# A hybrid decoder step on one core: three buffers for the weights' sums, written order on three engines, the first products of two units ahead

## The chip, the cores and the metric

The kernel runs on one core of a Trainium2 chip. The metric is the device time of one execution in microseconds (us), taken as the median of several runs. TensorE is called PE here, VectorE DVE, ScalarE ACT, GpSimd POOL and SyncE SP, as the profile names them. SP issues plain loads; POOL issues the loads that add to what is in memory already.

## The reference, cut to what matters

Two layers over 544 tokens (512 of a prompt and 8 times 4 of samples), model width 1024, all in float32. Each layer has two feed-forward blocks (FFN), so the step has four; between them stand a recurrent block, a shared key and value projection and differential attention. An FFN is the place of the change:

```python
def rmsnorm(x, g):
    xf = x.astype(jnp.float32)
    y = xf * lax.rsqrt(jnp.mean(xf * xf, axis=-1, keepdims=True) + EPS) * g.astype(jnp.float32)
    return y.astype(x.dtype)

def swiglu(x, w_gu, w_down):
    g, u = jnp.split(x @ w_gu, 2, axis=-1)
    return (jax.nn.silu(g) * u) @ w_down
...
        x = x + 0.5 * swiglu(rmsnorm(x, W['ffn1_norm'][i]), W['ffn1_w_gu'][i], W['ffn1_w_down'][i])
```

The hidden width `D_FF` is 2816, that is 22 slices of 128.

## The kernel before

**Tiling.** Activations lie with the 1024 channels on the 128 partitions in 8 blocks and the 544 tokens along the row. A float32 product is made of three products in the format float32r: a value is split into a high part (ACT casts it) and a low part (DVE subtracts the high part), and high by high, high by low and low by high are summed in PSUM.

**Units.** In the FFN one of the 22 slices is a unit `f`. Its gate and up products are written as seven products of half size (a Strassen-like scheme), each of 4 blocks by 3 splits = 12 matmuls of 272 columns. `s0` to `s6` issue them: on PE the order in the middle of a group is `s6(f)`, `s0(f+1)`, `s1(f)`, `s2(f+1)`, `s3(f+1)`, `s4(f)`, `s5(f+1)`, `s6(f+1)`, 84 matmuls for a unit. The seven products need sums of quarters of the weights. Tile `r` holds them: SP loads two quarters into it, POOL loads two others on top with an adding DMA, then DVE adds the quarters in `x` (loaded into a tile `raw`) by `sum6` (L427) and `sum3` (L432). So each unit has three weight operands, x, y and z, that are split in turn: `raw` is x, `r[:, 0:2]` is y (after `sum6`), `r[:, 2:4]` is z (after `sum3`); a fourth, `a`, is split into `w4`. The split is ACT `wh` (L370) and DVE `wl` (L371). Splits use three buffers in turn for x, y and z; `r` has two buffers.

**What follows a product on DVE.** L460 reads the sum of `s1(f)` out of PSUM, and PE's `s4(f)` adds to the same place only after that. L479 follows `s3`, L485 `s4`, L507 `s6`; L490 and L492 make the hidden slice, `hh` and `hl`.

**Groups.** The 22 units stand in three groups of 8, 7 and 7 (`DOWN`). After the units of a group come the down products: 8 output blocks, 384 or 336 matmuls (L211).

**Order.** A planner walks through `steps` and asks for loads and splits some units ahead (`pump`, `may_load`). From the code that results, a scheduler sets each engine's order by readiness and priority, so that an engine's instructions don't stand as they were written; an engine then runs its own in that order, and one that waits holds back all behind it.

**Start of an FFN.** `first_cycle` interleaves the products of unit 0 block by block, and `norm_done` makes the token's norm: squares summed on DVE or POOL, two times two matmuls with ones, then a chain of small DVE operations (`rsqrt_rows`, 13 on 17 columns, with a transposition ahead and a copy and a transposition behind) that ends in `rb`.

Of the kernel before, what the change touches and what calls it, by code (L numbers as in the profile page):

```python
# [8 lines left out]
F32 = mybir.dt.float32  # L9
# [66 lines left out]
def trunk_kernel(ctx: ExitStack, tc: tile.TileContext, I, O):  # L76
# [179 lines left out]
    def rsqrt_rows(out, ss, n, count, tr=None):  # L256

        nb = n // 32
        np_ = out.shape[0]
        if ss is not None:  # L260
            tr = npool.tile([P, T], F32, tag="tr", name="tr", bufs=1)[:, :n]
            norm["read"] = dve.transpose(tr, ss)
# [18 lines left out]

    def norm_done():
        if not norm["old"]:
            return
        norm["old"] = False
        hi = npool.tile([P, T], F32R, tag="sq", name="acch", bufs=1)
        lo = npool.tile([P, T], F32R, tag="tr", name="accl", bufs=1)
        split(hi, lo, norm["acc"])
# [5 lines left out]
        norm["ins"] = rsqrt_rows(rb, body(ps), T, D)  # L294
        norm["rb"] = rb
# [68 lines left out]
    def ffn(l, which, gain_out, spill_x=False, beside=None):  # L364
# [3 lines left out]

        def late_low(hi, lo, src):
            act.copy(hi, src)  # L370
            later(lambda: dve.tensor_tensor(lo, src, hi.bitcast(F32), op=OP.subtract))  # L371

# [21 lines left out]
        def unit_y(f):  # L394
            src = wgu[l, f]
            u = U[f]

            def load():
                r = u["r"] = F["w"].tile([P, 4, 512], F32, tag="r", name="r")
                sp.dma_start(r[:, 0:4:2, :], src[:, 1:3, :])  # L400
                pool.dma_start(r[:, 0:4:2, :], src[:, 0:2, :], accum_op=OP.add)  # L401
                u["a"] = F["w"].tile([P, 512], F32, tag="a", name="a")
                sp.dma_start(u["a"], src[:, 0, :])

            def cut():
                sum6(f)
                hi, lo = pair()
                late_low(hi, lo, u["r"][:, 0:2, :].rearrange("p k n -> p (k n)"))
                return hi, lo

            return {"load": load, "split": cut, "open": lambda: F.get("w") is not None}

        def unit_z(f):
            u = U[f]

            def cut():
                sum3(f)
# [4 lines left out]
            return {"load": lambda: None, "split": cut, "open": lambda: True}  # L422

# [10 lines left out]
        def low4(f):  # L434
            u = U[f]
            u["w4"] = [F["w"].tile([P, 512], F32R, tag=n, name=n, bufs=1) for n in ("w4h", "w4l")]
            late_low(*u["w4"], u["a"])

# [16 lines left out]
        def s1(f):  # L455

            u = U[f]
            product(u["b"], 7, ready[u["iz"]], 0, first=False)
            t1 = u["t1"] = F["w"].tile([P, T], F32, tag="t1", name="t1")
            dve.tensor_tensor(t1[:, TH:], u["b"], u["cc"][:, 2], op=OP.add)  # L460
            dve.tensor_tensor(t1[:, TH:], t1[:, TH:], norm["rb"][:, TH:], op=OP.mult)  # L461
            finish()

        def s2(f):
            u = U[f]
            u["c"] = new_ps()[:, :TH]
            product(u["c"], 5, ready[u["iy"]], 0)
            act.copy(u["cc"][:, 2], u["c"])
# [40 lines left out]

        def first_cycle(f):  # L510

            u = U[f]
            begin(f)
            u["c"] = new_ps()[:, :TH]
            for k in range(KC // 2):
                product(u["b"], 1, ready[u["ix"]], 0, [k])
                product(u["c"], 5, ready[u["iy"]], 0, [k])
            act.copy(u["cc"][:, 0], u["b"])  # L518
            act.copy(u["cc"][:, 2], u["c"])
            for k in range(KC // 2):  # L520
                product(u["a_"], 2, ready[u["ix"]], 512, [k])
                product(u["c"], 3, ready[u["iz"]], 512, [k], first=False)
                product(u["b"], 6, ready[u["iy"]], 512, [k], first=False)
            up_first(f)
            finish()
            act.copy(u["cc"][:, 1], u["b"])
            finish()
            dve.tensor_tensor(u["t2"][:, TH:], u["c"], u["cc"][:, 1], op=OP.add)
            low4(f)
            norm_done()  # L530

# [46 lines left out]
        def group(a, b):  # L578
            H["a"], H["b"] = a, b
            if a == 0:  # L580
                hp, H["close"] = open_pool("ffnh", bufs=1, side="right")
                H["hh"] = hp.tile([P, KC, T], F32R, name="hh")
                H["hl"] = hp.tile([P, KC, T], F32R, name="hl")

        def step(fn, *args):
            add(None, lambda: fn(*args), -1)

        for part, (a, b) in enumerate(DOWN):
            for f in range(a, b):
# [4 lines left out]
                if f == 0:  # L594
                    step(first_cycle, 0)
                    continue
                step(s0, f)
                if f > a:
                    step(s1, f - 1)
                step(s2, f)  # L600
                step(s3, f)
                if f > a:
# [4 lines left out]
            add(wdn[l, 0][:, a:b, :], down(0, part))  # L607
            step(s4, b - 1)
            step(down_rest, part)
            for m in range(1, KC):  # L610
                add(wdn[l, m][:, a:b, :], down(m, part))

# [359 lines left out]
    def shared_kv():  # L972
# [36 lines left out]
        def vstep(nh, kk):  # L1009
            def go(wh, wl):  # L1010
# [13 lines left out]
                for c in range(5):  # L1024
                    vo = pp.tile([P, 512], F32, tag="vo", name="vo")
                    dve.tensor_scalar(vo, banks[c], B["rt"][:, c : c + 1], None, op0=OP.mult)
# [561 lines left out]
    def start():  # L1588
# [16 lines left out]
        for k in range(KC):  # L1605
# [3 lines left out]
            if k == 3:  # L1609
                units[1]["load"]()  # L1610
        units[0]["take"](first[0])
        at["dma"], at["split"] = 3, 1
# [7 lines left out]
        for k in range(KC):  # L1620
# [3 lines left out]
            if k == 6:  # L1624
                split_unit()
        for k in range(KC):
            square_in(k, pool if k in () else dve)
        pool.dma_start(ident, cst("ident"))
# [81 lines left out]
    def may_load():  # L1710
# [140 lines left out]
```

## Time and profile before

| | |
|---|---|
| runs | 2444.92, 2446.29, 2449.08 us; median 2446.29 |
| the profiled execution's own time | 2453.01 us |
| its span | 2451.2 us |
| PE busy | 2183.6 us (89%) |
| DVE busy | 1537.3 us (63%) |
| ACT busy | 1056.9 us (43%) |
| mean granted PE clock | 0.946 |

The span runs from the first to the last instruction. Busy time of PE counts matmuls that overlap, so that a busy PE need not be one at its peak; the granted clock, in parts of full speed, says how fast they could run. What stands in the idle time of an engine is told by what ended it.

### The profile page before, as it was taken

The numbers are of one execution on the slowest core, as the hardware profiler recorded it, in microseconds if no ns is written. First come the engines' busy times: TensorE is split into PE (matmuls) and PEld (weight loads), VectorE is DVE, ScalarE is ACT, GpSimd is POOL, SyncE is SP. The second block draws the span as 40 slices with busy tenths as digits, with TensorE's granted clock in tenths as the row PEclk, the third lists the DMA queues.
The fourth block names the chain that finished last, engine by engine and source line by source line (L and its number), as shares of the span: only waits on it lengthen the run. The fifth ranks groups of instructions, "written<-read, shape, count | busy, mean of one in ns | idle before, by whom it ended". The sixth has DMA issues, their size and how long they took to land.

```text
span 2451.2 us, 39182 instructions
## 1 busy us (share of the span) xinstructions
PE 2183.6 (89%) x15973; PEld 2097.4 (86%) x15973; DVE 1537.3 (63%) x2516; ACT 1056.9 (43%) x1635; POOL 292.8 (12%) x307
## 2 busy tenths in 40 slices
PE   6898998999889899899988989899869889989897
PEld 5798998999879899899878979899736879889797
DVE  6665656777765565678566556567745665565676
ACT  5333424498443333445244243343644443333444
POOL 1000000222100000011000000003331100000012
PEclk7899999999989999999999999999989889999999
DMA  6543534336344454323674354438983445453331
GB/s 175 122 128 99 144 96 113 106 103 166 96 121 133 114 133 111 99 90 103 206 229 125 111 127 128 116 96 246 228 252 93 104 121 147 103 136 104 98 106 65
DMA packets 135636, 318.10 MB, mean 130 GB/s; under 512 B 13920, under 2 KB 25968, under 8 KB 135328
## 3 DMA queue, kind: packets, MB, share of 16 engines
q1 hardware_dynamic: 102432, 240.20, 31.1%
q0 software_dynamic: 32336, 74.80, 16.4%
q8 instruction: 125, 2.05, 0.3%
q10 hardware_dynamic: 688, 0.60, 0.1%
q14 instruction: 55, 0.45, 0.1%
HBM read 285.38 MB, written 17.58 MB: 124 GB/s over the span
## 4 chain that ended last, share of the span: by engine, by line
PE 46%; DMA 30%; DVE 15%; issue 5%; ACT 3%; POOL 0%; SPq 0%; POOLq 0%; DVEq 0%; ACTq 0%
PE ps L211 29%; DMA r<-in_ffn_gu 25%; PE ps L359 11%; DVE wl L371 3%; DVE r L427 2%; DVE r L432 2%; PE ps L1020 1%; PE g L211 1%; DVE t L460 1%; DMA x<-in_cache_v,idx 1%; DVE t L461 1%; DMA wl<-raw 1%; DVE wl L221 1%; DVE xgl L233 1%; DMA vt<-vscr 1%
## 5 line engine op out<-in xcount | busy, mean ns | idle before, releaser
L359 PE MATMUL ps<-xgh,wh 128*128 128x272 f32 x1408 | 414.9, 295 | 21.1 <-ACT cc L518 10.3
L359 PE MATMUL ps<-xgl,wh 128*128 128x272 f32 x1408 | 412.7, 293 | 5.7 <-DVE xgl L233 5.6
L359 PE MATMUL ps<-xgh,wl 128*128 128x272 f32 x1408 | 413.1, 293 | 4.5 <-DVE wl L371 4.3
L359 PEld LDWEIGHTS ps<-xgh,wh 128*128 128x128 f32 x1408 | 272.1, 193 | 23.7 <-ACT wh L370 11.2
L211 PE MATMUL ps<-hh,wl 128*128 128x256 f32 (+1 forms) x1408 | 291.6, 288 | 0.0
L211 PE MATMUL ps<-hh,wh 128*128 128x256 f32 (+1 forms) x1408 | 291.1, 288 | 0.0
L211 PE MATMUL ps<-hl,wh 128*128 128x256 f32 (+1 forms) x1408 | 290.8, 288 | 0.0
L427 DVE TENSOR_TENSOR r<-r,raw 128x512 f32<-128x512 f32 x88 | 62.0, 705 | 355.2 <-DMA r<-in_ffn_gu 254.6
L401 POOL DMA_DIRECT2D r<-in_ffn_gu x88 | 106.4, 1209 | 1459.9 <-DMA r<-in_ffn_gu 778.5
L359 PEld LDWEIGHTS ps<-xgl,wh 128*128 128x128 f32 x1408 | 272.0, 193 | 7.1 <-DVE xgl L233 7.1
L359 PEld LDWEIGHTS ps<-xgh,wl 128*128 128x128 f32 x1408 | 271.4, 193 | 5.9 <-DVE wl L371 5.5
L220 ACT CAST wh<-raw 128x1024 fp32r<-128x1024 f32 (+3 forms) x158 | 150.3, 959 | 270.7 <-PE ps L211 187.9
L371 DVE TENSOR_TENSOR wl<-r,wh 128x1024 fp32r<-128x1024 f32 x176 | 214.8, 1221 | 71.2 <-ACT wh L370 70.0
L359 PE MATMUL ps<-eh,w4h 128*128 128x272 f32 x352 | 121.7, 346 | 154.2 <-DVE t L460 154.1
L370 ACT CAST wh<-r 128x1024 fp32r<-128x1024 f32 x176 | 184.8, 1050 | 167.9 <-PE ps L359 87.7
L359 PE MATMUL ps<-eh,wh 128*128 128x272 f32 x704 | 223.4, 317 | 18.4 <-DVE t L479 13.6
L211 PEld LDWEIGHTS ps<-hl,wh 128*128 128x128 f32 x1408 | 226.8, 189 | 0.0
L211 PEld LDWEIGHTS ps<-hh,wh 128*128 128x128 f32 x1408 | 226.8, 189 | 0.0
L211 PEld LDWEIGHTS ps<-hh,wl 128*128 128x128 f32 x1408 | 225.4, 188 | 0.0
L359 PEld LDWEIGHTS ps<-eh,w4h 128*128 128x128 f32 x352 | 77.6, 220 | 167.4 <-DVE t L460 167.4
L359 PE MATMUL ps<-el,wh 128*128 128x272 f32 x704 | 216.3, 307 | 0.0
L359 PE MATMUL ps<-eh,wl 128*128 128x272 f32 x704 | 215.2, 306 | 0.0
(418 smaller groups left out, 4943.8 us busy)
## 6 DMA issues: line engine op xcount, KB each, us to landing
r<-in_ffn_gu SPq DMA_DIRECT2D x88, 512.0 KB, 3.8
r<-in_ffn_gu POOLq DMA_DIRECT2D x88, 512.0 KB, 6.8
raw<-in_ffn_gu SPq DMA_DIRECT2D x87, 512.0 KB, 4.1
raw<-in_ffn_dn SPq DMA_DIRECT2D x64, 448.0 KB, 4.0
a<-in_ffn_gu SPq DMA_DIRECT2D x88, 256.0 KB, 4.5
raw<-in_ffn_dn SPq DMA_DIRECT2D x32, 512.0 KB, 4.4
raw<-in_rg_in SPq DMA_DIRECT2D x16, 512.0 KB, 3.5
raw<-in_ple_gate SPq DMA_DIRECT2D x16, 512.0 KB, 3.4
```

The lines of the kernel that those rows point to most:

```text
L211: pe.matmul(ps[:, p0:p1], w[:, wc * P : (wc + 1) * P], a[:, k, t0:t1], start=first and q == 0 and s == 0, stop=last and q == n - 1 and s == 2,
L220: first = act.copy(hi, src)
L221: eng.tensor_tensor(lo, src, hi.bitcast(F32), op=OP.subtract)
L233: dve.scalar_tensor_tensor(lo, src, g, hi.bitcast(F32), op0=OP.mult, op1=OP.subtract)
L359: pe.matmul(ps, a[:, c0 + k * P : c0 + k * P + P], b, start=first and k == 0 and s == 0, stop=k == KC // 2 - 1 and s == 2, skip_group_chec ...
L370: act.copy(hi, src)
L371: later(lambda: dve.tensor_tensor(lo, src, hi.bitcast(F32), op=OP.subtract))
L401: pool.dma_start(r[:, 0:4:2, :], src[:, 0:2, :], accum_op=OP.add)
L427: u["s6"] = dve.tensor_tensor(u["r"][:, 1, :], u["r"][:, 0, :], u["x"][:, :512], op=OP.add)
L432: u["s3"] = dve.tensor_tensor(u["r"][:, 3, :], u["r"][:, 1, :], u["x"][:, 512:], op=OP.add)
L460: dve.tensor_tensor(t1[:, TH:], u["b"], u["cc"][:, 2], op=OP.add)
L461: dve.tensor_tensor(t1[:, TH:], t1[:, TH:], norm["rb"][:, TH:], op=OP.mult)
```

## The change

- `r` gets three buffers, and loads are asked for up to 9 operands ahead (6 before); `a` is loaded with operand z and no longer with y.
- From a group's first step to its last `s4`, PE, DVE and ACT keep the order in which the code is written (`manual_schedule`). `sum3(f+1)` is written ahead of `s1(f)`.
- `first_cycle` gives way to `first_products`, `second_products` and `first_rest`: of unit 0 and unit 1 all products that need no `e` (a sum of activations) come first (72 matmuls), then the norm's sums, then the rest.
- In the very first FFN the squares are not added up on DVE: ACT writes all 8, and PE sums them with 16 float32 matmuls (`ones` by `squares`).
- The tiles `vo` of the shared value projection lie in the FFN's pool.

```diff
-        ps = new_ps("ss")
-        for s, a in enumerate((hi, lo)):
-            for p0, p1, t0, t1 in HALF:
-                pe.matmul(ps[:, p0:p1], onesr, a[:, t0:t1], start=s == 0, stop=s == 1)
+        for out, (_, _, t0, t1) in zip(sums, HALF):
+            if squares is None:
+                for s, a in enumerate((hi, lo)):
+                    pe.matmul(out, onesr, a[:, t0:t1], start=s == 0, stop=s == 1)
+            else:
+                for k in range(KC):
+                    pe.matmul(out, ones, squares[:, k, t0:t1], start=k == 0, stop=k == KC - 1)
...
-                r = u["r"] = F["w"].tile([P, 4, 512], F32, tag="r", name="r")
+                r = u["r"] = F["w"].tile([P, 4, 512], F32, tag="r", name="r", bufs=3)
                 sp.dma_start(r[:, 0:4:2, :], src[:, 1:3, :])
                 pool.dma_start(r[:, 0:4:2, :], src[:, 0:2, :], accum_op=OP.add)
-                u["a"] = F["w"].tile([P, 512], F32, tag="a", name="a")
-                sp.dma_start(u["a"], src[:, 0, :])
...
         def s1(f):
 
             u = U[f]
+            if f + 1 < H["b"]:
+                sum3(f + 1)
             product(u["b"], 7, ready[u["iz"]], 0, first=False)
...
+        def second_products():
+
+            u = U[1]
+            while waiting:
+                flush()
+            begin(1)
+            ps = U[1]["pc"] = new_ps()
+            sums = (U[0]["pc"][:, 512 : 512 + TA], ps[:, 512 : 512 + TB])
+            product(u["b"], 1, ready[u["ix"]], 0)
+            act.copy(u["cc"][:, 0], u["b"])
+            product(U[0]["c"], 3, ready[U[0]["iz"]], 512, first=False)
+            product(u["a_"], 2, ready[u["ix"]], 512)
+            up_first(1)
+            norm_done(sums)
+
+        def first_rest():
+            u = U[0]
+            product(u["b"], 6, ready[u["iy"]], 512, first=False)
             act.copy(u["cc"][:, 1], u["b"])
+            dve.tensor_tensor(u["t2"][:, TH:], u["c"], u["cc"][:, 1], op=OP.add)
+            low4(0)
             finish()
...
             H["a"], H["b"] = a, b
+            H["order"] = tc.manual_schedule(engines={mybir.EngineType.PE, mybir.EngineType.DVE, mybir.EngineType.Activation})
+            H["order"].__enter__()
...
-            step(s4, b - 1)
-            step(down_rest, part)
+            step(s4, b - 1, hold=1)
+            add(None, lambda: H.pop("order").__exit__(None, None, None))
+            step(down_rest, part, hold=1)
...
         for k in range(KC):
-            square_in(k, pool if k in () else dve)
+            act.activation(norm["squares"][:, k, :], x[:, k, :], AF.Square)
...
-            return at["dma"] < at["split"] + 6 and u["open"]()
+            return at["dma"] < at["split"] + 9 and u["open"]()
```

**The middle of a group on DVE.** These rows are one unit of the first group, before; a row has the line, the operation, what it writes and reads, and the size. `wl<-r` is the low part of y or z, `wl<-raw` that of x, L427 is `sum6`, L432 `sum3`.

```order
L371 TENSOR_TENSOR wl<-r,wh 128x1024
L507 TENSOR_TENSOR t_952<-ps,cc 128x272
L492 TENSOR_TENSOR hl<-t_826,hh 128x544
L427 TENSOR_TENSOR r<-r,raw 128x512
L432 TENSOR_TENSOR r<-r,raw 128x512
L460 TENSOR_TENSOR t_1036<-ps,cc 128x272
L461 TENSOR_TENSOR t_1036<-t_1036,rb 128x272
L371 TENSOR_TENSOR wl<-r,wh 128x1024
L479 TENSOR_TENSOR t_1071<-ps,cc 128x272
L371 TENSOR_TENSOR wl<-raw,wh 128x1024
L485 TENSOR_TENSOR t_1036<-ps,rb 128x272
L371 TENSOR_TENSOR w4l<-a,w4h 128x512
```

The same stretch after the change; the lines have moved: L438 is `sum6`, L443 `sum3`, L473 follows `s1` (L460 before), L492 `s3` (L479), L498 `s4` (L485), L520 `s6` (L507), L505 makes `hl` (L492).

```order
L498 TENSOR_TENSOR t_914<-ps,rb 128x272
L380 TENSOR_TENSOR wl<-raw,wh 128x1024
L438 TENSOR_TENSOR r<-r,raw 128x512
L503 TENSOR_TENSOR t_829<-t_829,t_914 128x544
L520 TENSOR_TENSOR t_948<-ps,cc 128x272
L380 TENSOR_TENSOR wl<-r,wh 128x1024
L380 TENSOR_TENSOR w4l<-a,w4h 128x512
L443 TENSOR_TENSOR r<-r,raw 128x512
L473 TENSOR_TENSOR t_1033<-ps,cc 128x272
L474 TENSOR_TENSOR t_1033<-t_1033,rb 128x272
L505 TENSOR_TENSOR hl<-t_829,hh 128x544
L380 TENSOR_TENSOR wl<-r,wh 128x1024
```

`sum6` has left the place right ahead of `sum3` and of the read after `s1`; it now stands behind the read after `s4`, four instructions and a split ahead of that place.

**The start of the second FFN on DVE.** After the change, from the end of the norm's chain (L269, L270 write `rb`) to the first `wl` of unit 1's y; L566 is the read in `first_rest`.

```order
L269 COPY tr<-rs_y 128x544
L270 STREAM_TRANSPOSE rb<-tr 128x544
L566 TENSOR_TENSOR t_6436<-ps,cc 128x272
L438 TENSOR_TENSOR r<-r,raw 128x512
L380 TENSOR_TENSOR w4l<-a,w4h 128x512
L443 TENSOR_TENSOR r<-r,raw 128x512
L473 TENSOR_TENSOR t_6555<-ps,cc 128x272
L474 TENSOR_TENSOR t_6555<-t_6555,rb 128x272
L380 TENSOR_TENSOR wl<-r,wh 128x1024 x2
```

Before, the same work stood between the small operations of the chain (L246 to L252).

```order
L266 TENSOR_SCALAR rs_v<-tr 128x17
L427 TENSOR_TENSOR r<-r,raw 128x512
L246 TENSOR_SCALAR rs_h<-rs_v 128x17
L460 TENSOR_TENSOR t_6529<-ps,cc 128x272
L247 TENSOR_SCALAR rs_y<-rs_h 128x17
L432 TENSOR_TENSOR r<-r,raw 128x512
L248 TENSOR_SCALAR rs_h<-rs_v 128x17
L250 TENSOR_TENSOR rs_t<-rs_y 128x17
L371 TENSOR_TENSOR wl<-r,wh 128x1024
```

The chain was spread out among the sums and splits of unit 1; now it stands ahead of all of them.

**The loads on SP, in the second group.** Before:

```order
L400 DMA r<-in_ffn_gu 128x2x512
L382 DMA raw<-in_ffn_gu 128x1024
L400 DMA r<-in_ffn_gu 128x2x512
L382 DMA raw<-in_ffn_gu 128x1024
L403 DMA a<-in_ffn_gu 128x512
```

After:

```order
L409 DMA r<-in_ffn_gu 128x2x512
L431 DMA a<-in_ffn_gu 128x512
L391 DMA raw<-in_ffn_gu 128x1024
L409 DMA r<-in_ffn_gu 128x2x512
L431 DMA a<-in_ffn_gu 128x512
```

The three loads of a unit are the same, and `a` has moved from behind `raw` to behind `r`.

## Rows read from the trace of the kernel before

**Rows 1.** The page's head.

```profile
span 2451.2 us, 39182 instructions
```

**Rows 2.** Waits: who waited for whom, us in total, times, longest us.

```profile
PE ps L359 <- DVE t L460: 154.1, 59, 4.5
...
DVE r L427 <- DMA r<-in_ffn_gu: 254.6, 57, 6.4
```

**Rows 3.** Chain that ended last, inside the second group: start us, us, what.

```profile
225.11 0.70 DVE r L427
...
226.53 0.36 DVE t L460
...
227.35 1.14 DVE wl L371
...
228.52 3.88 DMA r<-in_ffn_gu
...
232.96 6.62 DMA r<-in_ffn_gu
239.61 0.70 DVE r L427
...
273.31 15.35 PE ps L359 x120
```

**Rows 4.** The same view, down products of the first group.

```profile
148.83 45.22 PE ps L211 x360
```

**Rows 5.** Windows, `s4` to `s4`: us, busy PE, PEld, DVE, ACT, POOL, PEclk, DMA share, GB/s.

```profile
211.00:226.90 15.90, 12.35 (x84) 12.13 (x84) 8.67 (x13) 6.02 (x9) 1.20 (x1) 0.89 0.48 117
226.90:241.40 14.50, 11.08 (x84) 10.64 (x84) 8.68 (x13) 5.91 (x9) 1.20 (x1) 1.00 0.50 127
...
271.30:282.50 11.20, 10.96 (x85) 10.74 (x86) 9.05 (x13) 4.88 (x8) 1.20 (x1) 1.00 0.64 159
```

**Rows 6.** Windows: second and third groups of the four FFNs, first row and sum.

```profile
194.10:468.30 274.20, 246.28 (x1850) 242.79 (x1849) 164.99 (x232) 107.16 (x156) 23.83 (x20) 0.96 0.43 113
...
sum 1095.80, PE 984.34 PEld 969.64 DVE 661.43 ACT 428.72 POOL 98.03; mean PE 246.09 PEld 242.41 DVE 165.36 ACT 107.18 POOL 24.51
```

**Rows 7.** Windows: the four first groups, sum.

```profile
sum 682.30, PE 587.50 PEld 573.67 DVE 426.53 ACT 268.17 POOL 44.29; mean PE 146.87 PEld 143.42 DVE 106.63 ACT 67.04 POOL 11.07
```

**Rows 8.** Windows: each FFN's first matmul to its first `s4`.

```profile
6.50:51.50 45.00, 22.38 (x113) 20.08 (x113) 34.48 (x64) 26.61 (x42) 4.26 (x4) 0.66 0.61 176
635.20:660.80 25.60, 19.25 (x114) 18.38 (x114) 19.78 (x34) 13.34 (x20) 2.56 (x2) 0.80 0.25 62
1242.80:1261.10 18.30, 15.25 (x109) 13.75 (x107) 10.94 (x17) 7.62 (x13) 1.20 (x1) 1.00 0.96 280
1932.80:1958.60 25.80, 19.31 (x114) 17.70 (x113) 20.66 (x36) 15.79 (x26) 2.71 (x2) 0.80 0.25 61
sum 114.70, PE 76.18 PEld 69.90 DVE 85.87 ACT 63.36 POOL 10.72; mean PE 19.05 PEld 17.48 DVE 21.47 ACT 15.84 POOL 2.68
```

**Rows 9.** Groups of instructions by line: xcount | busy us, mean ns | idle before.

```profile
L371 DVE TENSOR_TENSOR wl<-r,wh 128x1024 fp32r<-128x1024 f32 x176 | 214.8, 1221 | 71.2 <-ACT wh L370 70.0
L427 DVE TENSOR_TENSOR r<-r,raw 128x512 f32<-128x512 f32 x88 | 62.0, 705 | 355.2 <-DMA r<-in_ffn_gu 254.6 <-DMA raw<-in_ffn_gu 55.7 <-issue 44.9
L370 ACT CAST wh<-r 128x1024 fp32r<-128x1024 f32 x176 | 184.8, 1050 | 167.9 <-PE ps L359 87.7 <-PE ps L211 73.6 <-DVE r L427 3.1
L250 DVE TENSOR_TENSOR rs_t<-rs_y 128x17 f32<-128x17 f32 (+5 forms) x42 | 7.2, 172 | 0.7
L269 DVE STREAM_TRANSPOSE rb<-tr 128x544 f32<-128x544 f32 x8 | 6.0, 744 | 0.2
```

**Rows 10.** Timeline at the second FFN's start: start us, us, instruction.

```profile
644.78 0.78 DVE L233 SCALAR_TENSOR_TENSOR xgl<-x,vec,xgh 128x544 fp32r<-128x544 f32 x1
...
647.41 0.87 ACT L220 CAST eh<-e 128x816 fp32r<-128x816 f32 x1 [0.18 <-DVE e L336]
```

**Rows 11.** Timeline at the start: float32 matmuls that warm up PE.

```profile
1.07 5.49 PE L1619 MATMUL warm<-ones 128*128 128x128 f32 x24 [1.07 <-DVE ones L1614]
```

More of the change, by code (lines that the diff above doesn't have):

```diff
@@ L261, in rsqrt_rows @@
             tr = npool.tile([P, T], F32, tag="tr", name="tr", bufs=1)[:, :n]
-            norm["read"] = dve.transpose(tr, ss)
+            for a, t0, t1 in ss if isinstance(ss, list) else [(ss, 0, n)]:
+                dve.transpose(tr[:, t0:t1], a)
         var = npool.tile([P, 17], F32, tag="rs_v", name="rs_v")[:np_, :nb]
@@ L280, in square_in, with norm_done @@
         norm["old"] = True
[L282 to L292 removed]
+    def norm_done(sums=None):
+        squares = norm.pop("squares", None)
+        if squares is None:
+            if not norm["old"]:
+                return
+            hi = npool.tile([P, T], F32R, tag="sq", name="acch", bufs=1)
+            lo = npool.tile([P, T], F32R, tag="tr", name="accl", bufs=1)
+            split(hi, lo, norm["acc"])
+        norm["old"] = False
+        if sums is None:
+            ps = new_ps("ss")
+            sums = [ps[:, p0:p1] for p0, p1, _, _ in HALF]
+        for out, (_, _, t0, t1) in zip(sums, HALF):
+            if squares is None:
+                for s, a in enumerate((hi, lo)):
[3 more added lines that the diff above has]
+                    pe.matmul(out, ones, squares[:, k, t0:t1], start=k == 0, stop=k == KC - 1)
         rb = npool.tile([P, T], F32, tag="rb", name="rb", bufs=1)
[L294 removed]
+        norm["ins"] = rsqrt_rows(rb, [(out, t0, t1) for out, (_, _, t0, t1) in zip(sums, HALF)], T, D)
         norm["rb"] = rb
@@ L420, in cut, with load @@
                 return hi, lo
-            return {"load": lambda: None, "split": cut, "open": lambda: True}
+            def load():
+                u["a"] = F["w"].tile([P, 512], F32, tag="a", name="a")
+                sp.dma_start(u["a"], wgu[l, f][:, 0, :])
+            return {"load": load, "split": cut, "open": lambda: True}
         def sum6(f):
@@ L508, in s6, with first_products @@
             low4(f)
[L510 to L514, printed above, removed]
+        def first_products():
+            u = U[0]
+            while waiting:
+                flush()
+            begin(0)
+            u["pc"] = new_ps()
+            u["c"] = u["pc"][:, :TH]
             for k in range(KC // 2):
                 product(u["b"], 1, ready[u["ix"]], 0, [k])
-                product(u["c"], 5, ready[u["iy"]], 0, [k])
+                if "squares" not in norm:
+                    product(u["c"], 5, ready[u["iy"]], 0, [k])
             act.copy(u["cc"][:, 0], u["b"])
-            act.copy(u["cc"][:, 2], u["c"])
             for k in range(KC // 2):
                 product(u["a_"], 2, ready[u["ix"]], 512, [k])
-                product(u["c"], 3, ready[u["iz"]], 512, [k], first=False)
-                product(u["b"], 6, ready[u["iy"]], 512, [k], first=False)
-            up_first(f)
-            finish()
+                if "squares" in norm:
+                    product(u["c"], 5, ready[u["iy"]], 0, [k])
+                if k == 0 and "squares" not in norm:
+                    act.copy(u["cc"][:, 2], u["c"])
+            if "squares" in norm:
+                act.copy(u["cc"][:, 2], u["c"])
+            up_first(0)
+            finish()
+        def second_products():
+            u = U[1]
+            while waiting:
+                flush()
+            begin(1)
[8 more added lines that the diff above has]
+        def first_rest():
+            u = U[0]
+            product(u["b"], 6, ready[u["iy"]], 512, first=False)
             act.copy(u["cc"][:, 1], u["b"])
+            dve.tensor_tensor(u["t2"][:, TH:], u["c"], u["cc"][:, 1], op=OP.add)
+            low4(0)
             finish()
-            dve.tensor_tensor(u["t2"][:, TH:], u["c"], u["cc"][:, 1], op=OP.add)
-            low4(f)
-            norm_done()
         def down_part(m, part, ks, w, first, last):
@@ L594, in ffn @@
                 if f == 0:
-                    step(first_cycle, 0)
+                    step(first_products)
                     continue
-                step(s0, f)
+                if f == 1:
+                    step(second_products)
+                    step(first_rest)
+                else:
+                    step(s0, f)
                 if f > a:
@@ L1610, in start @@
                 units[1]["load"]()
+        units[2]["load"]()
         units[0]["take"](first[0])
```

24 lines of the change are left out of this document (13 added, 11 removed).

## The prediction, as it was put on record

> **What bounds the kernel now.** The span of the profiled execution is 2451.2 us [rows 1], and 1.8 lie around it. I read the table of waits first: on PE one wait stands out, for L460 on DVE, 154.1 us in 59 pieces [rows 2]. L460 is a short read; the reader should see in the second row that DVE itself waits at L427, `sum6`, for the adding load of `r`. The chain then shows why this repeats [rows 3]: the split of z (227.35) frees `r`, SP loads into it (228.52, 3.88 us), POOL adds on top (232.96, 6.62 us), `sum6` runs (239.61), then `sum3`, L460 and the next split of z. From one `sum6` to the next that is 239.61 - 225.11 = 14.5 us, of which 239.61 - 228.52 = 11.1 are the two loads. With two buffers each unit takes one such round.
>
> The windows show what this costs. The unit from 211.0 to 226.9 took 15.9 us, the one from 271.3 to 282.5, the last of its group, which has no next `sum6` to wait for, 11.2, both for 84 matmuls [rows 5]. PE without a wait needs 15.35 us for 120 matmuls of the products [rows 3], 128 ns each, and 45.22 us for 360 of the down products [rows 4], 125.6 ns. So a unit of 84 can take 10.75 us.
>
> A group of 7 at this pace is 7 x 10.75 + 336 x 0.1256 = 75.3 + 42.2 = 117.5 us. The eight second and third groups take 1095.8 us, 137.0 each [rows 6]. The first groups are longer and have a start of their own [rows 7, 8].
>
> **Term 1, the middle of the eight groups.** I walk one unit through the written order, from the start of `s6(f)` on PE as time 0; PE's products end at 1.5, 3.0 (`s0(f+1)`), 4.6 (`s1(f)`), 6.1, 7.7 (`s3(f+1)`), 9.2 (`s4(f)`), 10.7 (`s5(f+1)`). On DVE the read after `s4` can run at 9.3, the split of x until 10.9, `sum6(f+2)` until 11.6, the hidden product until 12.3, the read after `s6(f+1)` until 12.7. ACT's cast of y waits for `sum6` and takes 1.05, so the low part runs from 12.7 to 13.9; `w4l` 14.6, `sum3` 15.3, L473 15.7, one more half 16.1, `hl` 16.8, the split of z 18.0, the read after `s3` (PE ends it at 18.4) 18.8, and the next read after `s4` is due at 20.0. The durations are those of the rows by line (1.22, 0.70, 1.05) [rows 9], of L460's step in the chain (0.36, taken as 0.4) [rows 3], and 0.7 for the operations on 544 columns, as for `sum6`. PE wants L473 at 7.7 + 10.75 = 18.4 and gets it at 15.7; it wants y's low part at 15.6 and gets it at 13.9; it wants the read after `s3` at 20.0 and gets it at 18.8. Nothing on PE waits, with 1.2 us to spare at the tightest place. DVE works 8.67 us in a unit today, ACT 6.02 [rows 5], both under 10.75.
>
> The loads: buffer `r` of unit f comes free at 18.0 - 10.75 x 2 = -3.5, and `r(f+3)` is wanted at 11.6 - 0.7 + 10.75 = 21.7. That leaves 25 us for what takes 11.1 today. Loads get denser by 14.5/10.75, from a DMA share of 0.48 to 0.65, and one window shows 0.96 at 280 GB/s [rows 8], so the queue has room. That SP now issues `a` behind `r` makes `a` wait for `w4l(f)`, at 3.9, and with it the next `raw`; `raw(f+4)` is wanted two units later, so this costs nothing.
>
> At a group's start `s5` follows `s3` at once and waits for its read, 0.5 us. So 118 a group, a gain of 19.0, eight times: **-152**.
>
> Part of this gain is not idle time. Idle PE in these groups is only 1095.8 - 984.3 = 111.5 us [rows 6]; the rest is matmuls at the lower of the two clocks, 1.2 instead of 2.4 GHz: the unit with the stall shows a granted clock of 0.89 and 12.35 us busy, that without 1.00 and 10.96 [rows 5]. Counting idle time alone, the term would be -111. The Trainium skill, TensorE: Matmul & The Clock Gate, section on HAM oscillation, says that a wait in every turn of a loop sends the array back to the lower clock every time, and that keeping the array fed saves that too; the trace agrees (0.89 against 1.00), and by that rule the term is the -152.
>
> **Term 2, the first groups from their first `s4`.** 682.3 - 114.7 = 567.6 us today [rows 7, 8]. After: from `s4(0)` to `s4(7)` 6 x 84 + 72 = 576 matmuls at 128 ns, 73.7 us, then 12 + 360 at 125.6 ns, 46.7; 120.4 each, 481.7 for four. In the first FFN some 60 small DVE operations of the tables (0.17 us) stand among four units, ahead of their waits; DVE has 1.2 us spare a unit, so I add 3 (bounds 0 and 10, all of them on the path). **-83**.
>
> **Term 3, the starts.** Here I expect a loss. Unit 1's x takes the split buffer of unit 0's x, so it is cast only after the first 36 matmuls: 1.05 + 1.22, a wait of some 2.3. And y of unit 1 is split behind the norm's whole chain: transposition 0.74, 13 operations at 0.17 to 0.2, copy and transposition 1.4, then a read 0.4, `sum6` 0.7, `w4l` 0.7, `sum3` 0.7, L473 and L474 0.8, the split 1.2: 9.2 us, of which the 24 matmuls that PE has meanwhile cover 3.0. So PE waits 6.2 in the middle of the start. Second FFN: the last main operand ends at 645.56 and ACT is free behind `eh` at 648.28 [rows 10]; cast 649.4, low part 650.6, 34 matmuls, half of them at the lower clock for twice 126 ns, 657.0, the sums 657.5, chain 666.7, the last 10 matmuls 668.0. Today the first `s4` starts at 660.8 [rows 8]: +7. Fourth FFN by the same steps from its last operand: +8. Third: no norm chain, but the reads of `vo` hold DVE and ACT in order to about 1255, +9. First: the wait for x and y is the same as today, PE's float32 sums are added: 12 warm-up matmuls of 128 columns took 5.49 us [rows 11], at the lower clock 3.6 ns a column, at the higher 1.8; 8 x 544 columns are 7.8 us (15.6 at the lower). Against that DVE is spared 7 additions of squares, which stood beside waits that stay. I take +9. Together **+33**; the bounds are 0, if the products put first cover all of it, and 60, with the wait for y twice as long and the float32 sums at the lower clock.
>
> **Nothing elsewhere.** The other stretches keep their code. `vo` changes pool; two buffers as before.
>
> **The sum** against the profiled execution: 2451.2 + 1.8 - 152 - 83 + 33 = 2251. That execution lies 0.27% above the median of the runs, so 2251 x 2446.3/2453.0 = **2245 us**.
>
> **Rivals.** *DVE becomes the bound.* In written order DVE meets five reads a unit that wait for PE's ends, and each hand-over costs a little. For: 1.2 us to spare is little, 0.1 on each of 12 instructions eats it. Against: 8.67 us of work. If a unit takes 11.85, the 76 units that have a next one in their group cost 1.1 more: 2245 + 84 = 2329.
>
> *The split of y becomes the wait.* Its cast needs both `sum6` and the end of `s5`, stands on ACT between other work, and its low part has 1.7 us to spare. If PE waits 0.5 there each unit: +38, 2283. Short waits have not lowered the clock today (226.9 to 241.4, 14.5 us of which some 3 were waited, kept 1.00 [rows 5]), so only the wait counts.
>
> *The loads stay the bound, and the kernel is slower.* If `r` still comes late, `sum6` stands ahead of more work than before (the read after `s6`, the split of y, `w4l`, `sum3`, L473), units take 14 us again, terms 1 and 2 vanish and the starts' 33 remain: 2446 + 33 = 2479. It decides when the two loads of `r` together take over 25 us instead of 11.1. For: three units' loads in flight. Against: 0.65 of the DMA engines' time, and 0.96 seen.
>
> *The starts cost nothing.* The products put first would have to cover both splits and the norm's chain. For: they need no `e`, which today's start waits for. Against: the chain now stands ahead of the sums and splits of unit 1. -33: 2212.
>
> **How the numbers follow.** Forecast 0.66, its own range 2208 to 2275 (the starts' bounds and 10.55 to 10.9 for a unit); wait at y 0.13; DVE bound 0.11; starts for nothing, or better, 0.06; loads stay the bound 0.04. The range for 8 in 10 is 2200 to 2305: the forecast, the wait at y, the edge of both others. A measurement of this kernel tells 0.2% from no change, some 5 us. Faster 0.95, the same 0.01, slower 0.04.
>
> **What would show it.** In the changed kernel's profile the wait of PE for L473 is under 10 us in all; DVE's wait at L438 for the adding load is gone inside groups; windows from `s4` to `s4` are 10.6 to 11 us at a granted clock of 1.00; the eight groups take 118 each; the starts last longer, with PE waiting for the split of unit 1's x and y, and the float32 sums take 7 to 9 us. I am wrong if units take over 11.3 us, whoever is waited for, or if the starts lose more than 60 us.

## The result, and the profile after

The changed kernel takes 2253.76 us (median of 4 runs, 2246.61 to 2256.64); the kernel before, run beside it, 2447.53. The ratio is 0.9205, 95% interval [0.9181, 0.9229]. The forecast was 2245, with a range of 2200 to 2305. The profiled execution took 2252.29 us; the sum of the terms had put it at 2251.

The page of the changed kernel: the span, busy time by engine, and the chain that ended last by engine. PE is idle in 6% of the span, and the chain is mostly PE.

```profile
span 2250.4 us, 39241 instructions
PE 2114.8 (94%) x16001; PEld 2045.2 (91%) x16001; DVE 1532.9 (68%) x2516; ACT 1059.7 (47%) x1634; POOL 293.3 (13%) x307
...
PE 80%; DVE 7%; DMA 5%; ACT 4%; issue 3%; POOL 1%; SPq 0%; DVEq 0%; ACTq 0%; POOLq 0%
```

PE's waits in the changed kernel. The read L460 of [rows 2], now L473, is not among them; the longest is new, for the copy L535 (`cc` of a first product). On DVE `sum6`, now L438, waits for the adding load once, 5.1 us, where [rows 2] had 57 waits.

```profile
PE ps L368 <- ACT cc L535: 38.4, 4, 20.1
PE ps L368 <- ACT wh L379: 14.3, 8, 3.4
...
PE ps L368 <- DVE t L492: 4.8, 8, 0.6
```

Windows of the changed kernel, columns as in [rows 5]: one unit from `s4` to `s4`; the second and third groups (first row and sum, beside [rows 6]); the sum of the four first groups [rows 7]; the four starts up to the first `s4` [rows 8].

```profile
209.78:220.36 10.58, 10.58 (x87) 10.58 (x86) 8.69 (x13) 6.04 (x9) 1.20 (x1) 1.00 0.67 174
...
184.80:418.90 234.10, 232.89 (x1850) 232.46 (x1849) 165.99 (x235) 108.16 (x157) 22.61 (x19) 1.00 0.48 128
...
sum 936.60, PE 931.78 PEld 930.04 DVE 665.35 ACT 433.25 POOL 93.08; mean PE 232.94 PEld 232.51 DVE 166.34 ACT 108.31 POOL 23.27
...
sum 643.30, PE 571.28 PEld 560.84 DVE 420.74 ACT 266.86 POOL 46.62; mean PE 142.82 PEld 140.21 DVE 105.19 ACT 66.72 POOL 11.65
...
6.40:64.00 57.60, 27.80 (x141) 23.69 (x142) 33.56 (x77) 25.65 (x40) 5.46 (x5) 0.73 0.56 158
586.80:621.70 34.90, 21.42 (x113) 19.41 (x113) 22.16 (x43) 12.32 (x19) 2.57 (x2) 0.74 0.22 54
1144.70:1177.60 32.90, 18.22 (x109) 16.68 (x108) 12.99 (x19) 7.62 (x12) 2.34 (x2) 0.78 0.59 169
1784.50:1821.40 36.90, 22.84 (x112) 20.06 (x113) 27.37 (x52) 16.52 (x26) 2.70 (x2) 0.73 0.21 51
sum 162.30, PE 90.28 PEld 79.84 DVE 96.10 ACT 62.10 POOL 13.06; mean PE 22.57 PEld 19.96 DVE 24.02 ACT 15.53 POOL 3.27
```

A unit takes 10.58 us, PE works in all of it, and the granted clock is 1.00. A group takes 936.6 / 8 = 117.1 us instead of 137.0. The starts went the other way, 162.3 us instead of 114.7. The account of the span: middle groups -159.2; first groups from their first `s4` 643.3 - 162.3 = 481.0 instead of 567.6, -86.6; starts +47.6; all else -2.6; together -200.8.

The chain inside the second group has one piece, where [rows 3] had a round of loads, sums and splits:

```profile
195.96 36.12 PE ps L368 x287
```

### The profile page after: what moved, and what is told of

Read it like the earlier page. It is cut to its first block, busy times and chain, and to the rows that moved or that the text cites. A ratio compares the mean times of both kernels' runs of the same rounds, so it can differ in the third digit from the quotient of the medians.

```text
span 2250.4 us, 39241 instructions
## 1 busy us (share of the span) xinstructions
PE 2114.8 (94%) x16001; PEld 2045.2 (91%) x16001; DVE 1532.9 (68%) x2516; ACT 1059.7 (47%) x1634; POOL 293.3 (13%) x307
## 4 chain that ended last, share of the span: by engine, by line
PE 80%; DVE 7%; DMA 5%; ACT 4%; issue 3%; POOL 1%; SPq 0%; DVEq 0%; ACTq 0%; POOLq 0%
PE ps L368 41%; PE ps L211 32%; PE ps L1065 1%; PE g L211 1%; DMA out_v<-vo 1%; DMA r<-in_ffn_gu 1%; DVE wl L221 1%; DMA raw<-in_ffn_gu 1%; PE o L1466 1%; DMA wl<-raw 1%; DVE wl L380 1%; DMA vt<-vscr 1%; PE s L211 1%; DVE xgl L233 0%; PE S L1293 0%
## 5 line engine op out<-in xcount | busy, mean ns | idle before, releaser
L368 PE MATMUL ps<-xgh,wh 128*128 128x272 f32 x1408 | 417.1, 296 | 57.1 <-ACT cc L535 38.4
L379 ACT CAST wh<-r 128x1024 fp32r<-128x1024 f32 x176 | 185.2, 1052 | 190.5 <-PE ps L211 73.5
L368 PE MATMUL ps<-eh,wh 128*128 128x272 f32 x704 | 204.2, 290 | 6.7 <-DVE t L492 4.8
L368 PE MATMUL ps<-eh,wl 128*128 128x272 f32 x704 | 203.8, 290 | 0.0
L368 PE MATMUL ps<-el,wh 128*128 128x272 f32 x704 | 202.6, 288 | 0.0
L221 DVE TENSOR_TENSOR wl<-raw,wh 128x1024 fp32r<-128x1024 f32 (+3 forms) x158 | 176.0, 1118 | 35.3 <-ACT wh L220 34.5
L577 DVE SCALAR_TENSOR_TENSOR dn<-ps,rb 128x544 f32<-128x544 f32 x96 | 69.5, 724 | 169.0 <-PE ps L211 168.8
L379 ACT CAST wh<-raw 128x1024 fp32r<-128x1024 f32 x87 | 91.4, 1050 | 114.3 <-PE ps L368 76.7
```

The source lines that it names most:

```text
L221: eng.tensor_tensor(lo, src, hi.bitcast(F32), op=OP.subtract)
L368: pe.matmul(ps, a[:, c0 + k * P : c0 + k * P + P], b, start=first and k == 0 and s == 0, stop=k == KC // 2 - 1 and s == 2, skip_group_chec ...
L577: dve.scalar_tensor_tensor(t, body(ps), 0.5, norm["rb"], op0=OP.mult, op1=OP.mult)
```

## The experiments

### Which of the parts frees the middle: buffers or order

**The buffers alone** (`e1_buffers`): the kernel before, with

```
- r = u["r"] = F["w"].tile([P, 4, 512], F32, tag="r", name="r")
+ r = u["r"] = F["w"].tile([P, 4, 512], F32, tag="r", name="r", bufs=3)
- return at["dma"] < at["split"] + 6 and u["open"]()
+ return at["dma"] < at["split"] + 9 and u["open"]()
```

the load of `a` behind that of `r`, and `vo` in the tag `cc`, as in the change.

> The kernel before with the third buffer of r, the load distance of 9 and the load of a behind r alone; the scheduler sets the order on the engines as before, the starts and the squares are the old ones. My theory, that the round of the two loads of r bounded the unit: the wait of DVE for the adding load goes, units take 10.8 to 11.3 us instead of 14.5, the eight second and third groups 118 to 122 us each, the starts keep 45.0, 25.6, 18.3 and 25.8 us; 2446 - 152 - 83 = 2211, with 0.3 to 0.5 us a unit lost to the scheduler's order 2211 to 2250 us, so not slower than the whole change (2254). Rival, that the written order is what frees the loop: DVE meets its reads in the old order, PE still waits for L460, and the time stays at 2350 to 2446 us.

Measured: 2409.88 us, ratio 0.9857 [0.9819, 0.9896]; the eight groups sum to 1062.4 us instead of 1095.8. My theory fell. PE's longest wait and DVE's for the adding load stayed for the most part (154.1 and 254.6 us in [rows 2]):

```profile
DVE r L429 <- DMA r<-in_ffn_gu: 198.9, 45, 6.4
...
PE ps L359 <- DVE t L462: 118.6, 47, 4.4
```

Its chain in the second group shows the same round as [rows 3], with L429 and L434 the two sums, L462 the read that PE waits for and L371 the split of z:

```profile
209.18 8.08 DMA r<-in_ffn_gu
...
217.28 0.70 DVE r L429
...
218.01 0.69 DVE r L434
218.70 0.36 DVE t L462
...
219.53 1.14 DVE wl L371
...
220.69 3.81 DMA r<-in_ffn_gu
...
225.07 7.55 DMA r<-in_ffn_gu
...
232.65 0.70 DVE r L429
```

From sum to sum 232.65 - 217.28 = 15.4 us, with three buffers. What became of the third buffer is seen in DVE's order. Below, a row starts with its place in DVE's line, and tiles keep their buffer numbers; in this kernel L429 is `sum6` and the L371 with the same `raw` is the split of that unit's x:

```
409 L429 TENSOR_TENSOR r_3466<-r_3466,raw_3432 128x512
...
415 L371 TENSOR_TENSOR wl_3675<-raw_3306,wh_3674 128x1024
...
426 L371 TENSOR_TENSOR wl_3794<-raw_3432,wh_3793 128x1024
```

The sum stands 17 rows ahead of its own x's split; in the kernel before 6 rows (407 and 413), in the changed one right behind it. First the kernel before, then the changed one, each with the split of z of the unit in front (411 and 402):

```
407 L427 TENSOR_TENSOR r_3459<-r_3459,raw_3425 128x512
...
411 L371 TENSOR_TENSOR wl_3642<-r_3333,wh_3641 128x1024
...
413 L371 TENSOR_TENSOR wl_3675<-raw_3425,wh_3674 128x1024
```

```
402 L380 TENSOR_TENSOR wl_3644<-r_3218,wh_3643 128x1024
...
405 L380 TENSOR_TENSOR wl_3677<-raw_3308,wh_3676 128x1024
406 L438 TENSOR_TENSOR r_3342<-r_3342,raw_3308 128x512
```

So the change put `sum6` later in DVE's line and not earlier, as the sentence under the rows of the change can be read: the `sum6` that stood right ahead of the read L460 was the next unit's. A unit now holds its `r` for less time: from `sum6` to the split of its z 16.7 us before (225.11 to 241.77), 6.0 after (212.97 to 219.00). In the run with the buffers alone the scheduler used the third buffer to put `sum6` one unit further ahead, so that it again stands right behind the loads that the last split of z lets go, and ahead of the read that PE waits for.

**The order alone** (`e2_order2buf`): the changed kernel with `bufs=3` taken away again and `+ 9` set back to `+ 6`.

> The changed kernel with two buffers of r again and the load distance of 6. My theory, by the prediction's walk: a buffer of r comes free when z of its unit is split, and in the written order the next sum6 on this buffer runs 14.4 us later, for two loads that take 5.1 + 6.9 = 12.0 us from issue to landing in the changed kernel; so the loads just fit, units stay at 10.6 to 11.2 us, and the time is 2254 to 2300 us. Rival, that the third buffer is needed: the loads of two buffers come late by 1 to 3 us a unit, DVE waits for the adding load, the lower clock comes back, 76 units at 1.5 to 3.9 us more: 2370 to 2450 us.

Measured: 2243.35 us, 0.9176 [0.9141, 0.9211], which can't be told from the whole change. Its eight middle groups, sum:

```profile
sum 937.00, PE 932.18 PEld 930.26 DVE 665.32 ACT 433.49 POOL 97.57; mean PE 233.04 PEld 232.56 DVE 166.33 ACT 108.37 POOL 24.39
```

117.1 us a group with two buffers, as with three. In the written order the third buffer has no part in the gain; in the scheduler's order it came with 33 us (1062.4 against 1095.8). (Buffer and load distance were always changed together.)

**All but the order** (`e3_no_order`): the changed kernel without the two lines that enter and leave the written order.

> The changed kernel without the written order: code, buffers, products put first and TensorE's sums stay, the scheduler sets the order on PE, DVE and ACT. My theory, that buffers free the loop: groups of 117 to 122 us as in the changed kernel, and only the starts differ (the copy of the first product no longer stands behind ACT's other work, 38 us of waits in four starts): 2225 to 2275 us. Rival, that the order frees it: 2350 to 2450 us. Second rival: the scheduler's priorities put the products of the start elsewhere and the starts get longer than 57.6, 35.0, 32.9 and 36.9 us: 2275 to 2320 us.

Measured: 2414.3 us, 0.9874 [0.9836, 0.9912]; the rival held. The eight groups sum to 1060.7 us, 132.6 each, close to those with the buffers alone (132.8), and `sum6` stands 17 rows ahead of its own x's split here too.

**The order on DVE alone** (`e12_order_dve`):

```
- tc.manual_schedule(engines={mybir.EngineType.PE, mybir.EngineType.DVE, mybir.EngineType.Activation})
+ tc.manual_schedule(engines={mybir.EngineType.DVE})
```

> The changed kernel with the written order on DVE alone; PE and ACT take the scheduler's. My theory after the runs without the order: the middle of the groups is freed by the place of sum6 and sum3 in DVE's line (behind the split of x and ahead of the read after s1 of their own unit, not one unit earlier), so groups stay at 117 to 119 us; the starts lie between 121 and 162 us together; 2215 to 2265 us. Rival, that ACT's or PE's order matters as well: groups of 125 to 133 us and 2320 to 2410 us.

Measured: 2222.94 us, 0.9102 [0.9073, 0.9131]: faster than the whole change. The eight groups and then the four starts, sums:

```profile
sum 931.30, PE 931.30 PEld 929.71 DVE 663.38 ACT 433.11 POOL 93.63; mean PE 232.82 PEld 232.43 DVE 165.84 ACT 108.28 POOL 23.41
...
sum 136.70, PE 80.39 PEld 72.19 DVE 84.28 ACT 58.00 POOL 12.92; mean PE 20.10 PEld 18.05 DVE 21.07 ACT 14.50 POOL 3.23
```

PE idles nowhere in the eight groups. DVE's line is all that the middle needed; the order on PE and ACT returns nothing there, and the starts are 25.6 us longer with it (a little of this is that the scheduler puts the first `s4` some 8 to 10 matmuls sooner). No run moved `sum6` by itself: that its place is what counts in DVE's line is read from the chains and the rows. (DVE's order alone together with the late entry below was not tried.)

### What the walk left over: DVE's slack and the loads' slack

**More work on DVE** (`e7_dve_3`), results that nobody reads:

```
+ for _ in range(3):
+     dve.tensor_tensor(more, norm["rb"], norm["rb"], op=OP.mult)
  low4(f)
```

> The changed kernel with three more DVE operations of 0.7 us in each unit behind the read after s6, whose result nobody reads; a test of the walk, which leaves 1.2 us at its tightest place. The walk: 2.1 us more make the read after s3 0.9 us late in each unit, units take 11.5 us, some 76 units: 2254 + 68 = 2322 us, with PE waiting for the read behind s3 (L492). If only DVE's sum of work counts, 8.7 + 2.1 = 10.8 against 10.58 us: 0.2 us a unit, 2270 us. If each wait is a new one (clock of 0.9 as before): 2350 us or more.

Measured: 2313.97 us, 0.9473 [0.9443, 0.9502]. A unit, from one read after `s6` to the next, in its windows:

```profile
221.60:233.06 11.46, 10.85 (x87) 10.63 (x86) 10.58 (x16) 5.94 (x10) 1.20 (x1) 1.00 0.65 163
```

and DVE's timeline there: the three added operations, and behind them the split whose low part PE waits for (53.7 us in 80 waits, 0.61 each here).

```profile
221.96 2.23 DVE L523 TENSOR_TENSOR more<-rb 128x544 f32<-128x544 f32 x3
224.11 1.22 DVE L380 TENSOR_TENSOR wl<-r,wh 128x1024 fp32r<-128x1024 f32 x1
```

11.46 us against 11.5 expected: the added operations hold the split 224.11 - 221.96 = 2.15 us, of which 0.88 come through, so some 1.3 us were spare. The place was another than I said: not the read behind `s3` but the low part of y.

**One more load of r**, with three buffers (`e13_load_again_3`) and with two (`e14_load_again_2`); the same bytes are loaded twice:

```
  sp.dma_start(r[:, 0:4:2, :], src[:, 1:3, :])
+ pool.dma_start(r[:, 0:4:2, :], src[:, 1:3, :])
  pool.dma_start(r[:, 0:4:2, :], src[:, 0:2, :], accum_op=OP.add)
```

> The changed kernel with three buffers of r and one more load of r on POOL between the plain one and the adding one (the same bytes again). The loads of a unit's r then take some 5.4 + 6 + 6.5 = 18 us. My theory: with three buffers 25 us lie between the split of z and the next sum6 on the buffer, so nothing waits: 2254 to 2275 us. Rival: the DMA engines or POOL's line are what counts (0.5 MB more in each 10.6 us), loads of x and a come late as well: 2290 us or more.

> The same extra load with two buffers of r. My theory: 14.4 us are there for 18; a buffer's round is 18 + 6.8 us (sum6 to the split of z) for two units, 12.4 a unit instead of 10.6; 76 units: 2243 + 140 = 2383 us, up to 2450 with the lower clock, and DVE waits for the adding load at L438. Rival: the extra load is hidden here too, 2243 to 2275 us, and the number of buffers tells nothing.

Measured: 2262.69 us, 0.9266 [0.9237, 0.9295], with three buffers; 2441.09 us, 0.9992 [0.9975, 1.0009], with two. With three, the groups are untouched in the profiled execution (2253.77 us; the other three took 2262 to 2264, and where these 9 us lie is not shown):

```profile
sum 936.60, PE 931.78 PEld 930.04 DVE 664.50 ACT 433.09 POOL 126.62; mean PE 232.94 PEld 232.51 DVE 166.13 ACT 108.27 POOL 31.66
```

With two, DVE waits for the adding load again (L439 is `sum6` there), and the eight groups are as long as in the runs without the order:

```profile
DVE r L439 <- DMA r<-in_ffn_gu: 214.3, 58, 7.0
```

```profile
sum 1065.80, PE 984.01 PEld 969.09 DVE 662.11 ACT 426.73 POOL 133.59; mean PE 246.00 PEld 242.27 DVE 165.53 ACT 106.68 POOL 33.40
```

So the third buffer is a reserve: in the written order it is worth nothing while r's loads take some 12 us, and nearly the whole gain when one more load makes them too long for two buffers.

### What lengthens the starts

**The old start in the written order** (`e4_old_start`): `first_cycle` of the kernel before in place of `first_products`, `second_products` and `first_rest`; the low parts of units 0 and 1 follow one step behind the cast, as before.

> The changed kernel with the old start of an FFN (all products of unit 0 first, unit 1 as any other), in written order; TensorE still sums the squares. It prices term 3: the starts to the first s4 take 57.6, 35.0, 32.9 and 36.9 us in the changed kernel, 45.0, 25.6, 18.3 and 25.8 before, 47.7 us together. My theory, that the products put first cost this: 2254 - 48 = 2206 us, up to 2220 as the first FFN keeps TensorE's sums. Rival, that the written order lengthens the starts whatever stands in them (ACT and DVE meet waits in order): no gain, 2245 to 2290 us.

Measured: 2238.23 us, 0.9157 [0.9121, 0.9193]. The four starts, sum:

```profile
sum 156.40, PE 86.01 PEld 79.76 DVE 96.92 ACT 62.77 POOL 13.10; mean PE 21.50 PEld 19.94 DVE 24.23 ACT 15.69 POOL 3.27
```

156.4 us against 162.3. My theory fell: at most 6 us of the loss of 47.6 would come back, and even these can't be told, since the starts of the changed kernel, with the same code, sum to 154.8 us in the run with two buffers and to 165.8 in the one with one more load. Without the written order the products put first do cost something. The starts of the run without the order, which has them, sum to:

```profile
sum 137.20, PE 86.43 PEld 78.20 DVE 94.81 ACT 66.86 POOL 12.70; mean PE 21.61 PEld 19.55 DVE 23.70 ACT 16.72 POOL 3.18
```

With the buffers alone, which has the old start and no sums on TensorE, it is 121.3 us, some 16 less.

**The same, with the order entered only at the first `s4`** (`e9_order_from_s4`):

```
+ if f == 1:
+     add(None, order)
  if f > a:
      step(s4, f - 1)
```

where `order` holds the two lines that enter it; the second and third groups enter it at their start, as in the change.

> The changed kernel with the old start, and the written order of a first group entered only ahead of the first s4; until there the scheduler sets the order as before. My theory after the run with the old start (starts of 54.6, 33.4, 31.2 and 37.3 us to the first s4, 156.5 together, against 162.4 with the new one and 114.8 before): the written order itself lengthens the starts; with the scheduler's order they take some 121 us, as in the run with buffers alone, and the groups keep 117.2: 2254 - 41 = 2213 us. Rival, that the old start is short only where the scheduler also orders the units behind it (sums and splits of unit 1 and 2 put among the start): the wait comes at the seam, 2235 to 2250 us.

Measured: 2215.22 us, 0.9053 [0.9021, 0.9086]: faster than both kernels, 1.7% below the changed one by the ratios. The four starts:

```profile
6.30:45.40 39.10, 26.65 (x142) 22.18 (x141) 28.82 (x55) 25.74 (x41) 5.46 (x5) 0.78 0.80 230
566.50:592.70 26.20, 19.34 (x114) 18.36 (x113) 19.48 (x36) 14.41 (x22) 2.56 (x2) 0.74 0.25 61
1121.30:1148.70 27.40, 16.49 (x109) 15.83 (x108) 10.76 (x15) 7.26 (x12) 1.20 (x1) 0.81 0.65 193
1753.30:1780.10 26.80, 20.29 (x112) 18.69 (x113) 22.38 (x42) 16.17 (x26) 2.70 (x2) 0.75 0.24 60
sum 119.50, PE 82.77 PEld 75.06 DVE 81.44 ACT 63.58 POOL 11.91; mean PE 20.69 PEld 18.77 DVE 20.36 ACT 15.89 POOL 2.98
```

156.4 - 119.5 = 36.9 us are the written order's own with the old start, and 162.3 - 137.2 = 25.1 with the new one: order and products don't add up. The eight groups stay at 936.7 us. ACT's timelines in the first FFN show how. In the scheduler's order the cast of unit 1's y (`wh<-r`) runs at 38.18; in the written order, same code, at 52.09, since `sum6` of unit 1 stands behind the norm's chain on DVE. First the one with the late entry, then the one in written order throughout:

```profile
38.18 1.04 ACT L379 CAST wh<-r 128x1024 fp32r<-128x1024 f32 x1
```

```profile
52.09 1.04 ACT L379 CAST wh<-r 128x1024 fp32r<-128x1024 f32 x1 [10.59 <-DVE r L438]
```

**The copy behind the second product** (`e6_copy_later`) and, with it, **the norm's chain behind the split of y** (`e8_chain_later`), both in the changed kernel:

```
- act.copy(u["cc"][:, 0], u["b"])
  for k in range(KC // 2):
      product(u["a_"], 2, ready[u["ix"]], 512, [k])
...
+ act.copy(u["cc"][:, 0], u["b"])
```

```
- norm_done(sums)
+ norm_done(sums, wait=True)
```

with which the chain is issued in `s1(0)`, behind L473 and the low parts that are due.

> The changed kernel with ACT's copy of the first product of unit 0 issued behind the second product in place of ahead of it (L535 behind the loop of L536). My theory: PE waits 38.4 us at the four starts for this copy, since both products lie in one tile of PSUM; with the copy behind, the second product runs while ACT is busy, and unit 1's x can be split some 3 us earlier in each FFN; PE's wait then moves to that split. 2254 - 12 = 2242 us, and no wait for this copy on PE. Rival, that the row names the copy only because it came last, and PE waits for other operands (y, e) at the same time: no change, 2250 to 2258 us.

> The copy moved as in the run beside it, and the norm's chain on DVE (13 small operations, a copy, a transposition, 53.2 to 57.3 in the changed kernel's first FFN) put behind the split of unit 1's y instead of ahead of it. My theory, term 3's second part: PE waits 3.0 + 1.6 us for this split because the chain stands ahead of it on DVE; this falls to under 1 us in three of the four FFNs: 2242 - 11 = 2231 us. Rival: the chain is only moved, and holds the read behind s4(0) and the split of unit 2's x, so PE waits there instead: no gain over the moved copy, 2240 to 2246 us.

Measured: 2239.84 us, 0.9153 [0.9121, 0.9185], and 2232.49 us, 0.9123 [0.9093, 0.9153]. The starts sum to 151.6 and 145.4 us: 10.7 less than in the changed kernel (12 expected), and 6.2 less again (11 expected). Both together are clear of the changed kernel by their interval; each step by itself is not, beside starts that differ by 11 us for the same code. With the copy behind, PE no longer waits for it, but 36.7 us for the casts at L379 instead of 14.3: more than half of the 38.4 us was a wait for other work as well. With the chain behind too, a new wait takes part of the gain: the chain's transposition, now later, reads a tile that a product wants.

```profile
PE ps L375 <- DVE tr L263: 8.5, 3, 2.8
```

**The squares on DVE again** (`e5_squares_dve`):

```
- act.activation(norm["squares"][:, k, :], x[:, k, :], AF.Square)
+ square_in(k, pool if k in () else dve)
```

> The changed kernel with the first FFN's squares added on DVE again, as before; all else as changed. My theory, as the prediction has it: TensorE's float32 sums stand in PE's line (32 matmuls, 7.5 us, at 45.20 in the changed kernel) and the 7 additions of some 0.7 us that DVE is spared stood beside waits that stay, so the time falls by 6 to 7 us: 2247 us against 2254. Rival, that the additions hold DVE's splits of e and so the chain of ACT and DVE that PE waits for at 13.3 to 33.4: 5 us more ahead of PE's second product against 6.7 less behind it, no difference or slower: 2252 to 2260 us.

Measured: 2244.93 us, 0.9179 [0.9148, 0.9211]. The interval overlaps that of the change; the start that it touches takes 51.9 us instead of 57.6 (57.0 and 59.0 in the runs with two buffers and with one more load), -5.7, as my theory has it. That the sums cost this in the scheduler's order too is not shown: with the late entry they are in, and the first start takes 39.1, against 43.2 with the buffers alone, which has none. A run with the late entry and DVE's squares was not made.

## Why the prediction was right, and where it was not

**Term 1**, -152 forecast, -159.2 measured. Groups take 117.1 us instead of 118, since a product takes 10.58 / 84 = 126 ns and not 128; PE waits 0.6 us in each for the read behind `s3` (L492, 4.8 us in 8), as forecast with 0.5. The split into idle time and clock came out too: PE's idle time in these groups fell from 111.5 to 4.8 us, its busy time by 52.6, with the granted clock up from 0.96 to 1.00. Term 1 by idle time alone (-111) would have missed that third. The prediction put all of it down to the clock, and not all of it is: with more work on DVE the same groups show 944.4 us busy at a granted clock of 1.00, 12.6 more than here. The Trainium skill, TensorE: Matmul & The Clock Gate, section on HAM oscillation, says that a wait for a load in every turn of a loop brings the lower clock back each turn. The run with the buffers alone agrees in the main (idle 84.8 us in 1062.4, granted clock 0.95 to 0.97), though not for each turn: the unit at 226.90 in [rows 5] waited and kept 1.00. In the run with more work on DVE PE stopped for some 0.6 us a unit, and the granted clock stayed 1.00 in all eight groups.

**The cause named for it was wrong.** The failing step is "With two buffers each unit takes one such round". The round is real, but not the two buffers make it: three buffers have it too, and two in written order don't. What makes it is DVE's line, and by the rows the place of `sum6` in it: in the scheduler's order the next unit's `sum6`, which waits for loads that the last split of z let go, stands ahead of the read L460 for which PE waits, and ahead of the next split of z. The Trainium skill, PSUM — Partial Sum Buffer, section "Engine vs sequencer instructions", says that VectorE's queue is strictly first in, first out; by that a sum that waits for a load holds each read behind it, as the chain with the buffers alone shows (sum 217.28, read 218.70). My walk had the written order in it and so gave the right time; the sentence on the loads (25 us for what takes 11.1) gave the credit to the third buffer, where the 14.4 us of two would have done. I had the walk for that and did not make it.

**The loads' reserve** was sized rightly, as the two runs with one more load show: an estimated 18 us (5.4 + 6 + 6.5) fit into the time that three buffers leave (25) and not into that of two (14.4). The point from which the rival "The loads stay the bound" decides was not reached with three buffers.

**Term 2**, -83 forecast, -86.6 measured. The 3 us for the tables did not come: the first FFN's part is 178.4 - 57.6 = 120.8 us, the others' 119.5 to 120.4.

**Term 3**, +33 forecast, +47.6 measured, with each of the four starts 2 to 6 us longer than forecast. What it listed is there: the split of unit 1's x costs 1.4 + 0.7 us (2.3 forecast), the float32 sums 7.5 (7.8), and from their end to the end of y's split 52.7 to 61.5, 8.8 (9.2). But the loss is less that of the products put first, with which the step "Here I expect a loss. Unit 1's x takes the split buffer" begins, than of the written order, which costs 36.9 with the old start as well. Two things were not in the walk. First, the copy of the first product: in ACT's line it stands behind the casts and operands of the start, and PE's second product waits for it (38.4 us, of which moving it gave back 10.7 at most). The chain in the changed kernel, first FFN and third:

```profile
32.99 0.40 ACT cc L535
...
33.43 4.72 PE ps L368 x24
...
1152.22 6.01 DMA out_v<-vo
...
1158.33 0.40 ACT cc L535
...
1158.77 3.10 PE ps L368 x12
```

Second, the third FFN's rows: the copy waits for the store of `vo` to land. "`vo` changes pool; two buffers as before" is the failing step: `vo` now shares the tag `cc`, and unit 0's `cc` wants a buffer that the store still reads. In the scheduler's order too the third start is longer with `vo` there, 27.5 us with the buffers alone and 27.4 with the late entry against 18.3 in [rows 8], while the other three starts of these runs are at most 1.0 us longer than before; in the chains of both the store stands ahead of that copy (3.95 and 4.31 us). A run with `vo` alone moved back was not made, so the 9 us are argued and not shown.

**The sum.** -152 - 83 + 33 = -202 forecast, -200.8 measured; the misses of -7, -4, +15 and -3 (elsewhere) cancel. The forecast of 2245 was nearer than its parts deserve.

**Rivals.** DVE does not bind. The split of y is no wait, but it is the tightest place, with some 1.3 us spare, where the walk had 1.7; it gave its tightest place, 1.2, to the read behind `s3`. That the two figures lie close is chance. That the starts cost nothing did not come.

## What to carry to other kernels

Before a buffer is added for a load that comes late, read where its first reader stands in its engine's line: a scheduler can spend the buffer on moving that reader forward, and the wait stays. An order written out by hand pays in a loop that repeats, on the engine whose line is wrong; put over a start as well, it took back 25 to 37 us here. When a tile moves into another's tag, look whose waits it brings along; here the next user of the tag waited for a store.

## What the runs showed of the hardware

A short stop of PE in every turn cost no clock here: 0.61 us of 11.46 left the granted clock at 1.00 in all eight groups, while stops of up to 4.4 us, as in the run with the buffers alone, came with 0.95 to 0.97. A third load of `r` in each unit (0.5 MB more in 10.6 us, DMA share 0.55 instead of 0.48) changed nothing for PE in the eight groups as long as buffers were there. And in the changed kernel, where more loads are asked for ahead, the plain load of `r` took 5.1 us from issue to landing (median) against 3.8 before, the adding one 6.9 against 6.8; what slows the first was not taken apart.
